# Hybrid encoder layer with routed experts: the gate's weights loaded in the order of their use, and half a gather in other PSUM banks

## The chip, the cores and the metric

The kernel runs on one core of one Trainium2 chip. The metric is the device time of one execution in microseconds; lower is better. The engines are named as in the profile: PE is TensorE (PEld its weight loads), DVE is VectorE, ACT is ScalarE, POOL is GpSimd, SP is SyncE, which computes nothing and here issues the loads.

## The reference, cut to what matters

One layer over 256 tokens of width 2048, all in 32-bit floats. An input projection, attention and a state-space scan, an output projection and a layer norm come first; the change does not touch them. Then:

```
def routed_experts(x, w_router, router_bias, w_gate, w_up, w_down):
    ...                                     # sigmoid router, best group, top 2 of 16 experts per token
    for e in range(N_EXPERTS):
        hid = jax.nn.silu(xt @ w_gate[e]) * (xt @ w_up[e])
        out = out + combine[:, e:e + 1] * (hid @ w_down[e])
...
def per_layer_embedding(x, p_i, w_ple, w_ple_gate):
    gate = jax.nn.sigmoid(jnp.einsum('bsd,de->bse', x, w_ple_gate))
    return gate * jnp.einsum('bsk,kd->bsd', p_i, w_ple)
...
        h = layer_norm(DEEPNORM_ALPHA * h + moe + ple, ln2_g[i], ln2_b[i])
```

There are 16 experts with a hidden width of 1024: w_gate and w_up of an expert are 2048 x 1024 (8 MB each), w_down is 1024 x 2048 (8 MB). w_ple_gate is 2048 x 2048 (16 MB), w_ple is 256 x 2048 (2 MB).

## The kernel before, in words

After the first layer norm the transposed activations lie in `hT`, and the kernel walks through the experts 0 to 15. Each expert has room for 64 of the 256 tokens (`CAP`); tokens beyond that are counted, and an overflow loop behind a branch handles them. Per expert:

- `gate_up(e, xg)` (L724): the gathered tokens against w_gate and w_up, 8 tiles of 2 MB, 16 matmul instructions each;
- `hidden` (L734 to L750): silu and product, transposes; in its gaps stand the two halves of `return_half` of the expert before (L763 matmuls into banks named `bk`, then L768 on VectorE, which adds the weighted rows to `acc`). Its bank tags are mt and pl for the first half, gu and mt for the second;
- in experts 2, 4, 5 and 7 `residual` (L911 transposes into pl banks, L913 on VectorE);
- behind odd experts `gather` (L703): one-hot matmuls pick the tokens of the next two experts, into four PSUM tiles of which each is scaled and copied out by ScalarE or VectorE;
- `down(e, hidT)` (L790): 4 tiles of 2 MB; for the last expert `down_last` (L814) takes the weights in four quarters of 32 small DMAs in all;
- behind experts 3, 6, 9 and 12 `ple_gate(c)` (L832, L842): one of four column chunks of the per-layer gate, with 16 blocks of w_ple_gate in three ring tiles of 4, 8 and 4 blocks, the last with the chunk of w_ple.

In expert 7, between `residual` and `gather`, stands `overflow()`: the branch of L857 on a count that is read from memory. In expert 13 the gain and bias of the last norm are spread over the partitions by small matmuls (`row_bank`, L901).

All weights of the experts and of the gate come through one ring of SBUF buffers of 2 MB each (`class Ring`): eight from expert 1 on, and a ninth at the start. `plan_loads` writes the list of loads in order. `take` hands out a tile and puts its buffer in the list of spare ones, and `fill` issues the next loads of the list into spare buffers; both are called as the tiles are consumed, so the n-th load goes into the buffer of the n-8th tile taken, and SyncE waits with its DMA until TensorE has read that tile. SyncE issues in order. One gate chunk is five DMAs: four of 1 MB (L93) in rows of 2 KB, and one of 512 KB (L96). In the list the three tiles of a chunk stand ahead of the gate and up of the expert behind whose down they are used:

```
        if e in PLE_AT:
            c = PLE_AT.index(e)
            L += [(("pg", c, g), gate_part(g, c)) for g in range(3)]
        for k in range(4):
            L.append((("g", e, k), wide(i["w_gate"][0, e], k, R)))
            L.append((("u", e, k), wide(i["w_up"][0, e], k, R)))
```

The order on TensorE is written out by hand: `phase()` puts each of these parts behind the last TensorE instruction of the part before, except right behind the branch.

Of the kernel before, what the change touches and what calls it, by code (L numbers as in the profile page):

```python
# [7 lines left out]
F32 = mybir.dt.float32  # L8
# [10 lines left out]
NE, FE, CAP = 16, 1024, 64  # L19
# [4 lines left out]
WB = 3  # L24
RING0, RING1, RING2, RING3 = 4, 2, 2, 4
R = 4
PLE_AT = (3, 6, 9, 12)
RES_AT = (2, 4, 5, 7)
LN2_AT = 13
PLE_PARTS = ((0, 4), (4, 12), (12, 16))  # L30
# [43 lines left out]
def plan_loads(nc, ring, i):  # L74

    def rows(src, row0, nrow, col0, ncol):
        return lambda t: nc.sync.dma_start(
            t[:, :nrow // 128 * ncol].rearrange("p (k f) -> p k f", f=ncol),
            src[row0:row0 + nrow, col0:col0 + ncol].rearrange("(k p) f -> p k f", p=128))

    def wide(src, b, r):

        return lambda t: nc.sync.dma_start(t, src[b * 128 * r:(b + 1) * 128 * r, :].rearrange("(p r) f -> p (r f)", r=r))

    def gate_part(g, c):

        cs = slice(c * 512, (c + 1) * 512)
        k0, k1 = PLE_PARTS[g]

        def load(t):  # L90
            v = t.rearrange("p (k f) -> p k f", f=512)
            for k in range(k0, k1, R):
                nc.sync.dma_start(v[:, k - k0:k - k0 + R, :],  # L93
                                  i["w_ple_gate"][0][k * 128:(k + R) * 128, cs].rearrange("(p r) f -> p r f", r=R))
            if k1 == KB:
                nc.sync.dma_start(v[:, k1 - k0:k1 - k0 + 2, :], i["w_ple"][0][:, cs].rearrange("(k p) f -> p k f", p=128))  # L96
        return load

    def quarter(src, q):
        def load(t):  # L100
            v = t.rearrange("p (k d f) -> p k d f", d=2, f=256)
            for b in range(4):
                for dh in range(2):
                    nc.sync.dma_start(
                        v[:, 2 * b:2 * b + 2, dh, :],
                        src[b * 256:(b + 1) * 256, dh * 1024 + q * 256:dh * 1024 + (q + 1) * 256]
                        .rearrange("(p r) f -> p r f", r=2))
        return load

    L = ring.loads  # L110
    L.append(("p", rows(i["p"][0, 0], 0, 256, 0, 256)))
    for e in range(NE):
        if e in PLE_AT:
            c = PLE_AT.index(e)
            L += [(("pg", c, g), gate_part(g, c)) for g in range(3)]
        for k in range(4):
            L.append((("g", e, k), wide(i["w_gate"][0, e], k, R)))
            L.append((("u", e, k), wide(i["w_up"][0, e], k, R)))
        if e < NE - 1:
            L += [(("d", e, k), wide(i["w_down"][0, e], k, 2)) for k in range(4)]  # L120
        else:
            L += [(("d", e, q), quarter(i["w_down"][0, e], q)) for q in range(4)]


def front(ctx, tc, i, dbg=lambda *a: None):
# [6 lines left out]
    fr = Front()  # L132
    fr.const, fr.ring, fr.dram = const, ring, dram
    plan_loads(nc, ring, i)

    es_mix, es_xt, es_tm, es_ps = (ExitStack() for _ in range(4))
# [397 lines left out]
def back(ctx, tc, i, out, fr, dbg=lambda *a: None):  # L534
# [4 lines left out]
    psum = ctx.enter_context(tc.tile_pool(name="psum2", bufs=1, space=PSUM))  # L539
# [12 lines left out]
    def mt_psum(shape):  # L552
        return psum.tile(shape, F32, name="mt", tag="mt", bufs=2)
# [39 lines left out]
    for k2 in range(8):  # L593
        ps = banks[k2].rearrange("p (k t) -> p k t", k=2)
# [17 lines left out]
    for k in range(KB):  # L612
        g = k % 4
# [60 lines left out]
    @contextmanager  # L674
    def phase():

        after = tc.issue_after(place[0]) if place[0] else ExitStack()
        with after:
            yield
        place[0] = [i for i in nc.cur_bb.bb.instructions if i.engine == mybir.EngineType.PE][-1]  # L680
# [13 lines left out]
    def gather(oh):  # L694

        xg = mp.tile([128, KB, 2, CAP], F32, name="xg", tag="xg")
        for k4 in range(4):
            ps = mt_psum([128, 4, 2, CAP])
            ks = range(4 * k4, 4 * k4 + 4)
            for k in ks:  # L700
                cols = slice(k * 128, (k + 1) * 128)
                for t in range(NT):
                    nc.tensor.matmul(ps[:, k % 4], h[:, t, cols], oh[:, t], start=t == 0, stop=t == 1)  # L703
            if k4 % 2:
                for k in ks:
                    nc.scalar.activation(xg[:, k], ps[:, k % 4], AF.Identity, bias=lnT[:, 1, k:k + 1],
                                         scale=lnT[:, 0, k:k + 1])
            else:
                b = [128, 4, 2 * CAP]
                v, p = (a.rearrange("p k e c -> p k (e c)") for a in (xg[:, ks.start:ks.stop], ps))  # L710
                gain, bias = (lnT[:, n, ks.start:ks.stop, None].to_broadcast(b) for n in range(2))
                nc.vector.tensor_tensor(v, p, gain, op=OP.mult)
                nc.vector.tensor_tensor(v, v, bias, op=OP.add)
        return xg
# [110 lines left out]
    def ple_gate(c):  # L825
        cs = slice(c * 512, (c + 1) * 512)
        pg = [pl_psum() for _ in range(NT)]
        for g, (k0, k1) in enumerate(PLE_PARTS):
            w = v2(ring.take(("pg", c, g)), 512)
            for k in range(k0, k1):  # L830
                for t in range(NT):
                    nc.tensor.matmul(pg[t], hT[:, k, t * 128:(t + 1) * 128], w[:, k - k0, :],  # L832
                                     start=k == 0, stop=k == KB - 1)
            if k1 < KB:
                ring.fill()
        w = w[:, k1 - k0:k1 - k0 + 2, :]
        for t in range(NT):
            sg = mp.tile([128, 512], F32, name="sg", tag="w2", bufs=1)
            nc.scalar.activation(sg, pg[t], AF.Sigmoid)
            ps = mt_psum([128, 512])  # L840
            for k in range(2):
                nc.tensor.matmul(ps, pT[:, k, t * 128:(t + 1) * 128], w[:, k, :], start=k == 0, stop=k == 1)  # L842
            nc.vector.tensor_tensor(sg, sg, ps, op=OP.mult)
            nc.gpsimd.tensor_tensor(acc[:, t, cs], acc[:, t, cs], sg, op=OP.add)
        ring.fill()
# [48 lines left out]

    oh = onehot(0)
    xg = gather(oh)

    def row_bank(ps, rows, c):
# [17 lines left out]
    for e in range(NE):  # L916
# [18 lines left out]
        if e + 1 < NE:  # L935
            if e % 2:
                with phase():
                    oh = oh_next
                    xg = gather(oh)
            with phase():  # L940
                last = e, cm, down(e, hidT)
        else:
            with phase():
                down_last(e, hidT, cm)
        if e == 0:
# [16 lines left out]
            nc.gpsimd.dma_start(scro, ovT)  # L962
        if e in PLE_AT:
            with phase():
                ple_gate(PLE_AT.index(e))
        if e == LN2_AT:
# [50 lines left out]
```

## Time and profile before

| | us |
|---|---|
| median of 3 runs | 1493.62 |
| lowest and highest run | 1490.85, 1495.37 |
| the profiled execution | 1492.86 |
| its span, first to last instruction | 1490.7 |
| TensorE busy | 1369.6 |
| VectorE busy | 454.1 |
| ScalarE busy | 296.7 |
| GpSimd busy | 62.1 |

The span is that of one profiled execution; 2.2 us of its time lie outside. Busy times of engines overlap and don't add up to the span. The core read 496.68 MB from HBM, 335 GB/s over the span. Experts run from about 460 us to 1471 us.

### The profile page before, as it was taken

How to read it: one execution, taken by the hardware profiler on the slowest of the kernel's cores; microseconds unless marked ns; L12 is line 12 of the kernel's file. 1: busy time of each engine (PE TensorE's matmuls, PEld its weight loads, DVE VectorE, ACT ScalarE, POOL GpSimd, SP SyncE). 2: the span in 40 equal slices, each digit the busy share in tenths (PEclk: the TensorE clock that was granted, in tenths of full speed). 3: DMA queues.
4: the chain of work that ended last, by engine and by line, in shares of the span. 5: the costliest groups of instructions: out<-in, count | busy, mean ns of one | idle time of the engine just before them, and what ended most of it. 6: DMA issues, size and time to landing. Idle time of an engine off the chain costs nothing. (4 is left out here: it accounts for less than half of the span.)

```text
span 1490.7 us, 15640 instructions
## 1 busy us (share of the span) xinstructions
PE 1369.6 (92%) x6595; PEld 741.5 (50%) x6595; DVE 454.1 (30%) x768; ACT 296.7 (20%) x477; POOL 62.1 (4%) x80
## 2 busy tenths in 40 slices
PE   7999999999979999689998899897899988999994
PEld 5877888787765343144334233432443342335332
DVE  4486774545551022020113010320201111011127
ACT  3475554444330010010001000100100010002001
POOL 3000120200000000000000000000000000000002
PEclk9999999999998999899999999999999999999997
DMA  8655545466847999998899999899979999999994
GB/s 265 198 171 169 173 153 186 165 211 253 308 187 319 427 425 426 415 427 361 365 426 414 427 426 383 345 415 424 413 297 422 426 415 427 425 382 385 416 394 149
DMA packets 89647, 499.92 MB, mean 335 GB/s; under 512 B 9684, under 2 KB 22396, under 8 KB 65252
## 3 DMA queue, kind: packets, MB, share of 16 engines
q1 hardware_dynamic: 88128, 495.41, 82.9%
q0 software_dynamic: 1408, 3.41, 0.8%
q8 instruction: 54, 0.88, 0.2%
q14 instruction: 21, 0.17, 0.0%
q10 hardware_dynamic: 36, 0.05, 0.0%
HBM read 496.68 MB, written 2.16 MB: 335 GB/s over the span
## 5 line engine op out<-in xcount | busy, mean ns | idle before, releaser
L724 PE MATMUL pgu<-ring,xg 128*64 128x512 f32 x2048 | 458.5, 604 | 54.7 <-DMA ring<-in_w_gate 38.9
L724 PEld LDWEIGHTS pgu<-ring,xg 128*64 128x64 f32 x2048 | 148.1, 139 | 361.4 <-issue 315.1
L790 PE MATMUL py<-ring,hidT 128*64 128x512 f32 x960 | 210.2, 594 | 4.5 <-DMA ring<-in_w_down 3.5
L207 DVE TENSOR_TENSOR wl<-ring,wh 128x1024 fp32r<-128x1024 f32 x128 | 156.1, 1223 | 141.3 <-ACT wh L206 136.1
L206 ACT ACTIVATE wh<-ring 128x1024 fp32r<-128x1024 f32 x128 | 135.3, 1059 | 173.4 <-PE pj L213 145.0
L211 PE MATMUL pj<-wh,xh 128*128 128x512 f32 x384 | 153.9, 403 | 0.5 <-ACT xh L188 0.3
L212 PE MATMUL pj<-wl,xh 128*128 128x512 f32 x384 | 153.8, 401 | 0.0
L213 PE MATMUL pj<-wh,xl 128*128 128x512 f32 x384 | 152.9, 399 | 0.0
L734 DVE TENSOR_TENSOR hid<-hid,pgu 128x512 f32<-128x512 f32 x16 | 11.0, 687 | 433.2 <-ACT hid L733 433.2
L790 PEld LDWEIGHTS py<-ring,hidT 128*64 128x64 f32 x960 | 67.2, 137 | 137.4 <-issue 126.1
L832 PE MATMUL pl<-ring,hT 128*128 128x512 f32 x256 | 110.9, 594 | 0.0
L733 ACT ACTIVATE hid<-pgu 128x512 f32<-128x512 f32 x16 | 9.6, 597 | 424.5 <-PE pgu L724 424.5
L779 DVE TENSOR_TENSOR y<-py,y 128x512 fp32r<-128x512 f32 (+1 forms) x34 | 22.4, 660 | 220.0 <-ACT y L778 220.0
L703 PE MATMUL mt<-wr,h 128*128 128x128 f32 x512 | 67.5, 299 | 16.1 <-DVE acc L768 7.1
L768 DVE SCALAR_TENSOR_TENSOR acc<-bk,cw,acc 128x512 f32<-128x512 f32 (+1 forms) x128 | 81.7, 711 | 1.9 <-PE bk L763 1.9
L211 PEld LDWEIGHTS pj<-wh,xh 128*128 128x128 f32 x384 | 72.6, 189 | 17.5 <-ACT xh L188 1.5
L213 PEld LDWEIGHTS pj<-wh,xl 128*128 128x128 f32 x384 | 72.7, 189 | 16.5 <-DVE xl L189 0.2
L212 PEld LDWEIGHTS pj<-wl,xh 128*128 128x128 f32 x384 | 72.7, 189 | 16.1
L832 PEld LDWEIGHTS pl<-ring,hT 128*128 128x128 f32 x256 | 48.3, 190 | 62.6 <-issue 62.6
L703 PEld LDWEIGHTS mt<-wr,h 128*128 128x128 f32 x512 | 66.0, 212 | 18.6 <-DVE acc L768 8.9
L778 ACT ACTIVATE y<-py 128x512 fp32r<-128x512 f32 (+1 forms) x34 | 19.4, 572 | 234.6 <-PE py L790 206.0
L212 PE MATMUL pj<-wl,moh 128*128 128x512 f32 (+1 forms) x160 | 56.5, 353 | 0.5 <-DVE wl L207 0.5
(252 smaller groups left out, 933.9 us busy)
## 6 DMA issues: line engine op xcount, KB each, us to landing
ring<-in_w_gate SPq DMA_DIRECT2D x64, 2048.0 KB, 18.9
ring<-in_w_up SPq DMA_DIRECT2D x64, 2048.0 KB, 18.5
ring<-in_w_down SPq DMA_DIRECT2D x60, 2048.0 KB, 20.4
ring<-in_w_in SPq DMA_DIRECT2D x48, 1024.0 KB, 5.1
ring<-in_w_out SPq DMA_DIRECT2D x16, 1024.0 KB, 6.5
ring<-in_w_ple_gate SPq DMA_DIRECT2D x16, 1024.0 KB, 26.2
ring<-in_w_down SPq DMA_DIRECT2D x32, 256.0 KB, 6.0
xq<-in_x SPq DMA_DIRECT2D x8, 256.0 KB, 10.5
```

What stands on the lines that cost most here:

```text
L206: nc.scalar.activation(h, v, AF.Copy)
L207: nc.vector.tensor_tensor(l, v, h.bitcast(F32), op=OP.subtract)
L211: nc.tensor.matmul(ps, ah, bh, start=first, stop=False)
L212: nc.tensor.matmul(ps, ah, bl, start=False, stop=False)
L213: nc.tensor.matmul(ps, al, bh, start=False, stop=last)
L703: nc.tensor.matmul(ps[:, k % 4], h[:, t, cols], oh[:, t], start=t == 0, stop=t == 1)
L724: nc.tensor.matmul(pgu[j][hs], xg[:, k, e % 2, :], w[:, r, fh * 512:(fh + 1) * 512], start=k == 0, stop=k == KB - 1)
L768: nc.vector.scalar_tensor_tensor(a, ps[dh], cw[:, t, e:e + 1], a, op0=OP.mult, op1=OP.add)
L778: nc.scalar.activation(yh, ps, AF.Copy)
L779: nc.vector.tensor_tensor(yl, ps, yh.bitcast(F32), op=OP.subtract)
L790: nc.tensor.matmul(py[hs, c, :], hidT[:, j, fh * 64:(fh + 1) * 64], w[:, r, dh * 1024 + c * 512:dh * 1024 + (c + 1) * 512], start=fb == 0, ...
L832: nc.tensor.matmul(pg[t], hT[:, k, t * 128:(t + 1) * 128], w[:, k - k0, :], start=k == 0, stop=k == KB - 1)
```

## The change

The three tiles of a gate chunk are put in the list of loads behind the down tiles of the expert they follow, so that the list has the order of use. The chunks are behind experts 3, 7, 10 and 12 in place of 3, 6, 9 and 12 (counted from 0). Of gather's four PSUM tiles the first two take the banks with the tag pl, and the last two keep mt.

```
-PLE_AT = (3, 6, 9, 12)
+PLE_AT = (3, 7, 10, 12)
...
     for e in range(NE):
-        if e in PLE_AT:
-            c = PLE_AT.index(e)
-            L += [(("pg", c, g), gate_part(g, c)) for g in range(3)]
         for k in range(4):
             L.append((("g", e, k), wide(i["w_gate"][0, e], k, R)))
             L.append((("u", e, k), wide(i["w_up"][0, e], k, R)))
...
             L += [(("d", e, q), quarter(i["w_down"][0, e], q)) for q in range(4)]
+        if e in PLE_AT:
+            c = PLE_AT.index(e)
+            L += [(("pg", c, g), gate_part(g, c)) for g in range(3)]
...
         for k4 in range(4):
-            ps = mt_psum([128, 4, 2, CAP])
+            ps = psum.tile([128, 4, 2, CAP], F32, name="mt", tag=("pl", "mt")[k4 // 2], bufs=2)
```

## Rows read from the trace of the kernel before

**Rows 1.** The first part of the page: each engine's busy time, share of the span and instructions.

```profile
PE 1369.6 (92%) x6595; PEld 741.5 (50%) x6595; DVE 454.1 (30%) x768; ACT 296.7 (20%) x477; POOL 62.1 (4%) x80
```

**Rows 2.** TensorE's waits between 460 and 1466 us: what waited, for what, the total in us, how many times, the longest.

```profile
PE pgu L724 <- DMA ring<-in_w_gate: 38.9, 14, 13.2
PE pgu L724 <- DMA ring<-in_w_up: 15.8, 13, 1.3
PE mt L703 <- DVE acc L768: 7.1, 5, 1.9
PE mt L703 <- PEq L857: 6.1, 1, 6.1
PE py L790 <- DMA ring<-in_w_down: 3.5, 4, 1.3
```

**Rows 3.** Stretches of the span: from:to, length, then busy us and instructions of PE, PEld, DVE, ACT and POOL, and last the granted TensorE clock, the DMA engines' busy share and the GB/s they moved.

```profile
471.00:575.00 104.00, 101.10 (x522) 40.19 (x520) 14.72 (x26) 8.34 (x18) 0.62 (x1) 1.00 1.01 426
536.90:544.40 7.50, 7.48 (x66) 7.36 (x68) 3.72 (x7) 1.50 (x4) 0.00 (x0) 1.00 1.00 426
575.00:655.00 80.00, 60.13 (x280) 20.36 (x275) 11.10 (x17) 3.26 (x6) 0.00 (x0) 0.91 1.01 421
600.30:612.30 12.00, 3.87 (x20) 1.11 (x16) 1.38 (x2) 1.19 (x2) 0.00 (x0) 0.83 1.06 401
697.00:718.00 21.00, 21.00 (x62) 8.56 (x62) 1.38 (x2) 1.19 (x2) 2.52 (x2) 1.00 0.55 201
900.00:910.00 10.00, 10.00 (x34) 3.85 (x34) 1.38 (x2) 1.19 (x2) 2.54 (x2) 1.00 0.70 264
952.00:962.00 10.00, 10.00 (x58) 4.96 (x59) 1.38 (x2) 1.97 (x6) 0.00 (x0) 1.00 0.37 125
1062.20:1071.40 9.20, 9.13 (x66) 9.01 (x68) 3.77 (x8) 1.50 (x4) 0.00 (x0) 0.81 1.00 424
1090.00:1120.00 30.00, 30.00 (x80) 12.75 (x80) 1.37 (x2) 1.19 (x2) 2.53 (x2) 1.00 0.66 258
1300.00:1314.00 14.00, 14.00 (x45) 5.57 (x45) 1.38 (x2) 1.19 (x2) 3.50 (x4) 1.00 0.77 304
1374.00:1382.00 8.00, 8.00 (x36) 2.42 (x34) 0.00 (x0) 0.00 (x0) 0.00 (x0) 0.86 0.54 186
```

**Rows 4.** TensorE in order of time, experts 2 to 4 and the start of 10 and 11: start, length, line, operation and shapes, in brackets the idle time before and what ended it.

```profile
558.12 27.64 PE L724 MATMUL pgu<-ring,xg 128*64 128x512 f32 x128
590.22 13.95 PE L790 MATMUL py<-ring,hidT 128*64 128x512 f32 x64
...
651.64 3.65 PE L724 MATMUL pgu<-ring,xg 128*64 128x512 f32 x16 [1.25 <-DMA ring<-in_w_up]
...
682.04 27.73 PE L832 MATMUL pl<-ring,hT 128*128 128x512 f32 x64
713.14 27.69 PE L724 MATMUL pgu<-ring,xg 128*64 128x512 f32 x128
...
1116.29 27.69 PE L724 MATMUL pgu<-ring,xg 128*64 128x512 f32 x128
...
1161.20 27.64 PE L724 MATMUL pgu<-ring,xg 128*64 128x512 f32 x128
```

**Rows 5.** SyncE's issues in order of time, around the first chunk: start, the time that the issuing took, line and DMA.

```profile
575.50 24.01 SPq L93 DMA_DIRECT2D ring<-in_w_ple_gate  x4
...
602.16 1.18 SPq L83 DMA_DIRECT2D ring<-in_w_gate  x1
...
689.21 0.33 SPq L83 DMA_DIRECT2D ring<-in_w_up  x1
702.94 0.33 SPq L83 DMA_DIRECT2D ring<-in_w_gate  x1
713.24 0.33 SPq L83 DMA_DIRECT2D ring<-in_w_up  x1
```

**Rows 6.** The loads that L83 issues between 700 and 715 us, from issue to landing.

```profile
DMA to landing us min/median/max: 7.9/7.9/7.9
```

**Rows 7.** The branch's line on SyncE and on TensorE's sequencer: how many, the shortest, median and longest in ns, first and last start in us.

```profile
L857 SPq EVENT_SEMAPHORE  x8: 17/17/17, 945.1 to 955.1; - x8
L857 PEldq COMPARE_BRANCH  x1: 6172/6172/6172, 938.1 to 938.1; - x1
```

**Rows 8.** TensorE in order of time: the first instruction behind gate and up of expert 7, and the first of expert 8.

```profile
933.99 1.19 PE L763 MATMUL bk<-y,cm 64*128 64x512 f32 x8
...
968.28 27.64 PE L724 MATMUL pgu<-ring,xg 128*64 128x512 f32 x128
```

**Rows 9.** TensorE before and at the gather of expert 9, VectorE's accumulations at the same time, and VectorE's residual of expert 5, in order of time.

```profile
1059.13 1.19 PE L763 MATMUL bk<-y,cm 64*128 64x512 f32 x8
1062.27 9.11 PE L703 MATMUL mt<-wr,h 128*128 128x128 f32 x64 [1.95 <-DVE acc L768]
...
1057.52 5.36 DVE L768 SCALAR_TENSOR_TENSOR acc<-bk,cw,acc 128x512 f32<-128x512 f32 x8
...
792.69 2.08 DVE L913 SCALAR_TENSOR_TENSOR acc<-pl,acc 128x512 f32<-128x512 f32 x2
```

**Rows 10.** TensorE in order of time: the start of the last chunk's matmuls as far as the asked stretch goes, and the last quarter of the last down.

```profile
1278.47 21.73 PE L832 MATMUL pl<-ring,hT 128*128 128x512 f32 x50
...
1465.70 3.67 PE L814 MATMUL py<-ring,hidT 128*64 128x256 f32 x32
```

## The prediction

> **What bounds the kernel now.** I read the page first. TensorE is busy for 92% of the span [rows 1], which looks like the bound, but pipelined matmuls make that share hard to read. So I went to TensorE's waits in the expert stretch, 460 to 1466 us [rows 2]. It waited 38.9 + 15.8 + 3.5 = 58.2 us for weights that were still being loaded, 7.1 us for VectorE's accumulations, and 6.1 us once at the branch of the overflow code. So weights are what it lacks. The third view asks whether the DMA engines were full all that time [rows 3]. In long stretches they move 421 to 426 GB/s at a share of 1.0, the most that any row of the page shows. But in six short stretches they don't. Against 425 GB/s the lost DMA time is length x (1 - rate/425): 697 to 718 loses 11.1 us, 900 to 910 3.8, 952 to 962 7.1, 1090 to 1120 11.8, 1300 to 1314 4.0, 1374 to 1382 4.5; together 42.2 us. Four of the six lie at the four chunks of the per-layer gate (at 682 to 713 for the first, [rows 4]), one at the overflow branch, one near the end.
>
> So the expert stretch is bound by DMA, and its engines stop now and then because no buffer is free. While the first chunk runs, SyncE issues a load only as the chunk's parts are consumed: 689.2, 702.9, 713.2 us [rows 5]. That is the wait to read the change by.
>
> **A rule for the loss, checked on the old order.** The ring has eight 2 MB buffers; a load goes out when the tile eight takes earlier has been read. A tile is 2.10 MB / 426 GB/s = 4.92 us. A load into an idle queue lands after 7.9 us [rows 6], so a restart costs 7.9 - 4.9 = 3.0 us. A chunk holds TensorE for 713.14 - 682.04 = 31.1 us, and hands back its three buffers 6.9, 20.7 and 31.1 us after its start [rows 4, 5]. Let L be the lead: how long before a chunk starts the last down tile ahead of it has landed. In the old order the chunk's three tiles were loaded a whole expert earlier and sit in three buffers, so behind that down tile the queue has five buffers and the first two that the chunk frees: 7 x 4.92 = 34.4 us. The third can restart it at L + 31.1 + 0.1 + 3.0 = L + 34.2. Loss = L - 0.2.
>
> Where the gate and up before was starved, the last up tile is picked up as it lands. For expert 3 that is 651.6; the chunk starts 30.4 us later, the four down tiles take 19.7, so L = 10.7 and the loss 10.5 (measured 11.1). Behind expert 9 the same, with a gather 1.6 us slower: 12.1 (measured 11.8). Behind 6 and 12 even the down tiles were awaited, L = 3.5, loss 3.3 (measured 3.8 and 4.0). Four chunks, 29.2 by the rule and 30.7 by the trace.
>
> **The change, part by part.**
>
> *Loads behind the down.* No transfer is added or removed. The 20 DMAs of the four chunks (16 gate, 4 projection) move on SyncE's queue past the twelve loads of their expert; POOL's queue is untouched. Loads now stand in the order of use, so the chunk itself is still on its way when the last down tile has landed: 4.72 MB at 401 GB/s is 11.8 us [rows 3]. Loss = L - 12.0, or nothing below that.
>
> *Chunk behind expert 3 (index as in the code).* Its gate and up are starved (expert 2 ends at 604, and 39.4 us of tiles face 27.6 us of matmuls), so L is 10.7 again, or 8.8 with the gather's wait gone. Loss 0, with 1.3 to 3 us to spare. The 13.2 us wait before expert 3 [rows 2], when TensorE sat behind the chunk's transfer, shrinks as well.
>
> *From there to the second chunk.* After a chunk the lead is L + 31.1 - 11.8, some 28 to 30. An expert's twelve tiles need 59 us. TensorE needs 44.9 for an even expert (1116.29 to 1161.20), 46.0 with a residual (558.12 to 604.17), 54.4 for an odd one [rows 4]. The lead goes to about 16, 11 and then under zero: expert 6 is starved, and so is the gate and up of 7.
>
> *Chunk behind expert 7, past the overflow branch.* From the end of gate and up to the end of the down is 968.28 - 933.99 = 34.3 us there [rows 8], the 6.2 us branch included [rows 7]; with the last up tile's own 3.6 us, less 19.7, L = 18.2. And SyncE drains: after the branch it passes eight waits between 945.1 and 955.1 us, the last as the last load lands [rows 7], and issues nothing before. In the new order the last load ahead of the branch is the first gate tile of expert 8, which lands 11.8 + 4.9 us after the down tiles, 1.5 us before the chunk starts. Restart: 0.4 + 3.0 = 3.4 us lost. Then four down buffers and two parts of the chunk, 6 x 4.92 = 29.5 us, last to 31.4 us into the chunk, and the third part restarts at 34.2: 2.8 lost. Together 6.2 us, in place of 7.1 for the branch alone now.
>
> *Chunks behind 10 and 12.* By the same ledger the lead is 17 after expert 8, 11 after 9, and 10 is starved: L = 3.5, loss 0. Then 23, 16 after 11, about 2 after 12: starved again, loss 0. The 4.5 us at 1374 go too: a full ring stood still there while TensorE was at LN2's row banks; by the ledger the lead behind expert 13 is about 27 us, of the 39 that eight buffers can hold.
>
> *Half of the gather in other banks.* Gather's first bank now waits for the seventh of eight VectorE accumulations: matmuls end at 1060.3, it starts at 1062.27, 1.9 us [rows 9]; and two of those gathers then ran 1.6 us longer: a granted clock of 0.81 in the one at 1062, in part the level of 1.2 GHz, after that pause, against 1.00 (2.4 GHz) in the one at 537 [rows 3]. The pl banks are free after the fourth accumulation, about 1060.2. Gain 1.9 us at experts 1, 3, 9 and 11, and up to 3.3 of clock: at most 11 us of TensorE time. At expert 5 the residual's two VectorE operations (792.69 to 794.8) hold pl instead: about 1.7 us worse, where the first operation ends at 793.8. All of it lies behind DMA, so it counts nothing in the sum; without that cover it would be -9 us. Bounds: -9 and +2.
>
> **Sum.** 42.2 - 6.2 = 36.0 us. The rule came out 1.5 us low over four chunks, so I take 35. Does TensorE become the bound at the end? Its work from the last chunk on runs without a wait for weights today, from 1278.47 [rows 10]. That chunk would start 11.8 (its own transfer no longer stands ahead) + 33.8 (the first four losses) - 6.2 = 39.4 us earlier, so TensorE alone would end at 1490.7 - 39.4 = 1451.3, and DMA, at 1490.7 - 35 = 1455.7, ends last. The tail behind the last quarter of the down, 1490.7 - 1465.7 = 25.0 us, stays. The profiled execution has 2.2 us outside its span and lies 0.8 us under the median of the runs, so 1455.7 + 2.2 + 0.8 = 1458.7 us.
>
> **A rate from the Trainium skill.** Two stretches of 80 and 104 us ran at 421 and 426 GB/s [rows 3]. The Trainium skill's page "HBM Reference", section "Specifications (TRN2)", gives a core a share of about 358 GB/s when both cores of a pair stream, and says that one alone measures about 425. By the share, the 401 MB behind 471 us would take some 1120 us where 994 are used now, an estimate from that page; the trace agrees with the figure for a core alone.
>
> **Rivals.**
> *Slower: issuing the chunk starves the queue.* SyncE spent 24.0 us on four gate DMAs, against 0.3 for a weight tile [rows 5], and can issue nothing else meanwhile. If the queue ran dry behind each, every chunk could cost up to 24 us, 4 x 24 - 35 = 61 slower (1555); it decides from 35/4 = 8.8 us a chunk on, and at 11 a chunk the time is 1503. For it: the chunk now comes when the queue is short. Against it: in 575 to 655, with that issue inside, the DMA share is 1.01 [rows 3], and the same four down tiles stand ahead of it. 5 in 100.
> The Trainium skill's page "Perfetto Trace Analysis", section 'What "DMA-bound" means', names this case: an issuing engine solid with DMA slices is the bound. Here the slices are solid, but the engines behind them are full, so the trace does not bear it out.
> *The branch costs more.* If the drain kept SyncE from issuing until the second chunk has freed its last buffer, the queue would stand 34 us in place of 6: 1487. If TensorE had to wait out SyncE's drain too, some 22 us: 1481. Today TensorE left the branch at 944.4 while SyncE drained to 955.1 [rows 7], which speaks against it. 9 in 100.
> *No change.* TensorE, not DMA, would have to set the time. 58 us of its waits are for DMA, so it can't hold over the whole stretch; 3 in 100, at 1493.6.
> *More than forecast.* The join costs nothing and TensorE's end decides: 1451 to 1454. 8 in 100.
>
> **How the numbers follow.** The forecast has 75 in 100, by itself 1454 to 1466 (a few microseconds of idle where 1.3 us of slack runs out, and 4 us of TensorE surprise hidden). The range 1451 to 1471 takes in the better case and small excess at the branch. A change of 0.3%, 4.5 us, is about what a measurement of this kernel can tell from none. Faster: 75 + 8 + 9 = 92; same 3; slower 5.
>
> **What would show it.** Right: the DMA rate stays at 420 or more through the chunks behind 3, 10 and 12; one gap of 3 to 4 us after the branch and one of about 3 at the end of the chunk behind 7; TensorE's waits for the ring fall from 58 to 30 to 45 us and lie in experts 3, 6, 7, 10 and 15; gathers start without the 1.9 us wait, except behind the residual of 5. Wrong: a DMA gap behind the gate issues, TensorE waiting at the branch until SyncE has drained, or no ring wait left at the end.

## The result and the profile after

| | before | after |
|---|---|---|
| median of the runs, us | 1494.21 (4 runs) | 1453.22 (4 runs) |
| lowest and highest run, us | 1490.85, 1495.37 | 1453.09, 1454.92 |
| the profiled execution, us | 1492.86 | 1453.28 |
| its span, us | 1490.7 | 1451.2 |

The ratio is 0.9732, with a 95% interval of 0.9714 to 0.975: faster by 2.7%. The forecast was 1458.7 us with a range of 1451 to 1471; the time came out 5.5 us below the forecast, inside the range. A second set of runs of the same kernel gave 1453.0 us and 0.9731 [0.9717, 0.9744].

The first part of the page after, beside [rows 1]: each engine runs as many instructions as before, and TensorE's share rose although its busy time fell by 11.2 us, because the span shrank by 39.5.

```profile
PE 1358.4 (94%) x6595; PEld 735.2 (51%) x6595; DVE 453.5 (31%) x768; ACT 296.9 (20%) x477; POOL 62.1 (4%) x80
```

TensorE's waits from 460 to 1430 us, beside [rows 2] (what waited, for what, total us, times, longest):

```profile
PE pgu L724 <- DMA ring<-in_w_up: 18.2, 16, 1.3
PE pgu L724 <- DMA ring<-in_w_gate: 14.9, 13, 1.3
PE py L790 <- DMA ring<-in_w_down: 6.4, 7, 1.3
PE mt L703 <- PEq L857: 6.1, 1, 6.1
...
PE mt L703 <- DVE acc L768: 0.9, 1, 0.9
```

The waits for weights fell from 58.2 to 18.2 + 14.9 + 6.4 = 39.5 us. The 13.2 us wait is gone: the longest left for weights is 1.3. Of the gathers' waits for VectorE, 7.1 us, one of 0.9 is left. TensorE still lacks weights, but each time only by the little that a full queue brings them late.

Whether the queue is full is to be seen in stretches of the span, beside [rows 3] (from:to, length, busy us and instructions of PE, PEld, DVE, ACT and POOL, granted clock, DMA share, GB/s):

```profile
471.00:575.00 104.00, 103.04 (x530) 40.78 (x528) 14.54 (x26) 8.35 (x18) 0.62 (x1) 1.00 1.01 427
655.00:700.00 45.00, 45.00 (x140) 18.12 (x138) 2.76 (x4) 2.40 (x4) 2.01 (x2) 1.00 1.02 417
700.00:900.00 200.00, 177.25 (x894) 67.76 (x890) 40.95 (x64) 12.48 (x26) 0.52 (x1) 1.00 1.01 427
920.00:932.00 12.00, 12.00 (x42) 4.63 (x39) 1.38 (x2) 1.20 (x2) 0.00 (x0) 1.00 0.66 251
952.00:962.00 10.00, 10.00 (x39) 3.62 (x39) 1.38 (x2) 1.20 (x2) 2.53 (x2) 1.00 0.86 336
1100.00:1140.00 40.00, 38.70 (x108) 15.86 (x106) 2.76 (x4) 2.39 (x4) 1.89 (x2) 1.00 1.02 415
1230.00:1270.00 40.00, 38.65 (x108) 15.86 (x106) 2.07 (x3) 2.35 (x4) 2.25 (x3) 1.00 1.02 416
1320.00:1345.00 25.00, 25.00 (x132) 13.90 (x130) 1.39 (x2) 5.76 (x10) 0.00 (x0) 0.86 1.01 427
1345.00:1399.00 54.00, 53.26 (x262) 18.56 (x260) 8.08 (x12) 2.67 (x5) 0.00 (x0) 1.00 1.01 427
```

Through the chunks behind experts 3, 10 and 12 (655 to 700, 1100 to 1140, 1230 to 1270) the engines are full; the 415 to 417 GB/s at a share of 1.02 are the chunk's own slower rows of 2 KB, which moved at 401 in [rows 3]. The stretch behind LN2's row banks, which lost 4.5 us from 1374 to 1382 before, now lies some 40 us earlier and is full too (1320 to 1345), like the one behind it. Two gaps are left, where the forecast put them: 920 to 932, behind the overflow branch, and 952 to 962, at the end of the chunk behind expert 7.

### The profile page after: what moved, and what is told of

Read it like the earlier page. It is cut to its first block, busy times and chain, and to the rows that moved or that the text cites. A ratio compares the mean times of both kernels' runs of the same rounds, so it can differ in the third digit from the quotient of the medians.

```text
span 1451.2 us, 15673 instructions
## 1 busy us (share of the span) xinstructions
PE 1358.4 (94%) x6595; PEld 735.2 (51%) x6595; DVE 453.5 (31%) x768; ACT 296.9 (20%) x477; POOL 62.1 (4%) x80
## 5 line engine op out<-in xcount | busy, mean ns | idle before, releaser
L724 PE MATMUL pgu<-ring,xg 128*64 128x512 f32 x2048 | 450.2, 595 | 33.1 <-DMA ring<-in_w_up 18.2
L779 DVE TENSOR_TENSOR y<-py,y 128x512 fp32r<-128x512 f32 (+1 forms) x34 | 22.5, 660 | 223.8 <-ACT y L778 223.8
L703 PE MATMUL mt<-wr,h 128*128 128x128 f32 x512 | 64.0, 289 | 7.9 <-PEq L857 6.1
L703 PEld LDWEIGHTS mt<-wr,h 128*128 128x128 f32 x512 | 62.5, 204 | 10.3 <-PEq L857 6.3
## 6 DMA issues: line engine op xcount, KB each, us to landing
ring<-in_w_down SPq DMA_DIRECT2D x60, 2048.0 KB, 25.8
```

The source lines that it names most:

```text
L724: nc.tensor.matmul(pgu[j][hs], xg[:, k, e % 2, :], w[:, r, fh * 512:(fh + 1) * 512], start=k == 0, stop=k == KB - 1)
L779: nc.vector.tensor_tensor(yl, ps, yh.bitcast(F32), op=OP.subtract)
```

## The experiments

**The parts alone.** Four kernels divide the change: the new order of the loads alone, the new places alone, the new banks alone, and the whole change without the banks.

The order alone, as an edit of the kernel after:

```
-PLE_AT = (3, 7, 10, 12)
+PLE_AT = (3, 6, 9, 12)
...
-            ps = psum.tile([128, 4, 2, CAP], F32, name="mt", tag=("pl", "mt")[k4 // 2], bufs=2)
+            ps = mt_psum([128, 4, 2, CAP])
```

> The loads in the order of use alone: chunks behind 3, 6, 9 and 12 as before, gather in its old banks. Theory (order): the old order lost 30.7 us at the chunks because three buffers held a chunk for a whole expert; with the order alone the loss at the chunks is L - 12.0, L about 10.7 behind 3, 12.3 behind 9, 3.5 behind 6 and 12, so almost nothing, and the branch costs one restart of 3 us with no chunk right behind it. 1449 to 1455 us. Rival (TensorE): the pauses before the gathers and the slower clock set a good part of the time; without the new banks it is 9 to 11 us above the changed kernel, 1462 to 1464. Rival (places): the chunk must stand behind 7 and 10; at 1465 or above if that is worth a third of the gain.

Measured: 1452.34 us, ratio 0.9735 [0.9719, 0.9752], the same as the whole change. Stretches of its span, columns as above; the overflow branch is in the second, and the third is the end of the chunk behind expert 3, where the first gap of [rows 3] stood:

```profile
900.00:930.00 30.00, 24.01 (x148) 15.16 (x145) 11.53 (x18) 2.98 (x7) 0.00 (x0) 0.89 1.01 423
930.00:950.00 20.00, 20.00 (x98) 7.03 (x98) 1.56 (x3) 2.70 (x6) 0.00 (x0) 1.00 0.80 322
690.00:712.00 22.00, 22.00 (x76) 8.44 (x76) 1.38 (x2) 1.19 (x2) 2.53 (x2) 1.00 1.00 416
```

One gap is left, behind the branch: 20 x (1 - 322/425) = 4.8 us. The order alone carries a gain as large as the whole. The rivals by which TensorE or the places would have held part of it fall.

The places alone, as an edit of the kernel before:

```
-PLE_AT = (3, 6, 9, 12)
+PLE_AT = (3, 7, 10, 12)
```

> Only the chunks' places are new (behind 3, 7, 10 and 12); loads in the old order, gather in its old banks. Theory (order): nothing gained, since a chunk still holds three buffers for an expert; the chunk behind 7 now stands right after the branch's drain, so its loss is not smaller: 1492 to 1498 us. Rival (places): below 1485.

Measured: 1492.49 us, ratio 1.0002 [0.999, 1.0013]. The places do nothing in the old order.

The banks alone, as an edit of the kernel before:

```
-            ps = mt_psum([128, 4, 2, CAP])
+            ps = psum.tile([128, 4, 2, CAP], F32, name="mt", tag=("pl", "mt")[k4 // 2], bufs=2)
```

> Only the gather's banks are new, loads and places as before. Theory (order): in the old order the loss at a chunk is L - 0.2, and L falls by the 1.9 us wait (and 1.6 of clock) behind the odd experts 3 and 9, so this edit, which should be nearly worthless in the new order, gains some 5 to 9 us in the old: 1485 to 1489 us, with a smaller DMA gap at the chunks behind 3 and 9 and unchanged ones behind 6 and 12. Rival (TensorE): every pause counts, 9 to 11 us: 1483 to 1485, DMA gaps smaller everywhere. If it is hidden here too: 1492 to 1496.

Measured: 1486.01 us, ratio 0.9952 [0.9935, 0.997]. Its stretches at the chunks behind experts 3, 6 and 9, beside [rows 3]:

```profile
695.00:716.00 21.00, 21.00 (x64) 8.53 (x64) 1.38 (x2) 1.19 (x2) 2.52 (x2) 1.00 0.64 239
898.00:908.00 10.00, 10.00 (x35) 3.72 (x35) 1.38 (x2) 1.20 (x2) 2.54 (x2) 1.00 0.69 259
...
1086.00:1116.00 30.00, 30.00 (x83) 12.58 (x83) 1.38 (x2) 1.19 (x2) 2.54 (x2) 1.00 0.72 284
```

In the old order a faster gather did count, and the rule for the loss says where: a gather stands between the last up tile's pick-up and the chunk only behind odd experts, and only there does a faster gather shorten the lead L. Behind 3 the loss is 21 x (1 - 239/425) = 9.2 us in place of 11.1, behind 9 it is 30 x (1 - 284/425) = 10.0 in place of 11.8; behind 6, with no gather ahead of the chunk, it is 3.9, as before (3.8). That is the size of the rule behind 3 (1.9 us) and half of it behind 9, where it has 3.5. These two account for 3.7 us. The span of the profiled execution fell by 5.0, of which 1.2 is an earlier start of the first expert (458.69 us in place of 459.86). The runs fell by more, 6 to 7 us (1486.01 against a median of 1492.18 in the same set, and by the ratio); what lies beyond the 5.0 no profile here shows.

The whole change without the banks, as an edit of the kernel after:

```
-            ps = psum.tile([128, 4, 2, CAP], F32, name="mt", tag=("pl", "mt")[k4 // 2], bufs=2)
+            ps = mt_psum([128, 4, 2, CAP])
```

> The changed kernel with the gather back in its old banks. Theory (order): hidden behind DMA, 0 to 2 us above the changed kernel's 1453.2: 1453 to 1455. Rival (TensorE): 9 to 11 above, 1462 to 1464.

Measured: 1455.29 us, ratio 0.9753 [0.9737, 0.977], just over the expected stretch; the interval overlaps that of the kernel after. Its profiled span is 1451.9. Its waits from 460 to 1430 us:

```profile
PE pgu L724 <- DMA ring<-in_w_up: 11.9, 10, 1.3
PE pgu L724 <- DMA ring<-in_w_gate: 10.3, 9, 1.3
PE mt L703 <- DVE acc L768: 7.1, 5, 1.9
PE mt L703 <- PEq L857: 5.8, 1, 5.8
PE py L790 <- DMA ring<-in_w_down: 3.6, 4, 1.3
PE mt L703 <- DVE acc L770: 1.9, 1, 1.9
```

TensorE waits 25.8 us for weights in place of 39.5, 13.7 less, and the span is 0.7 us longer: it spends about as much more on its own, 8.1 us in the gathers' waits for VectorE (7.1 + 1.9 in place of 0.9) and 5.8 in slower gathers (L703 is busy for 69.8 us in place of 64.0). That is the cover of which the prediction spoke, seen from the other side: once the DMA engines are full, what TensorE saves it waits out again. The banks are worth 6 to 7 us where gaps stand behind a lead, and some 2 us (1455.29 against 1453.22), not told from nothing by the intervals, where none does.

**The places in the new order.** An edit of the kernel after:

```
-PLE_AT = (3, 7, 10, 12)
+PLE_AT = (3, 6, 9, 12)
```

> The changed kernel (order of use, new banks) with the chunks back behind 3, 6, 9 and 12. Theory (order): the chunk behind 7 costs about 2 us of DMA at its end, since the ring had only just restarted after the branch; without it there the branch costs its restart of 3 us alone. 1449.5 to 1453.5 us, 0 to 3 under the changed kernel's 1453.2. Rival (places): 1457 or above.

Measured: 1453.68 us, ratio 0.9742 [0.9721, 0.9764], just over the expected stretch and not to be told from the kernel after. The places are neutral here too.

**The branch.** The overflow loop is left out of both kernels:

```
-OV_AT = 7
+OV_AT = 99
```

> The changed kernel without the overflow branch (the loop for tokens beyond an expert's capacity is left out). Theory: the branch costs DMA 3 us of restart and 2 us at the end of the chunk behind it, and TensorE 6.1 us that lie behind DMA; 1447 to 1450 us, both DMA gaps gone. Rival: the branch costs only TensorE's 6.1 us, or nothing: 1453.

Measured from the kernel after: 1448.19 us, ratio 0.97 [0.9676, 0.9723], 5.0 us less than after. Stretches of its span:

```profile
905.00:935.00 30.00, 30.00 (x101) 11.80 (x98) 1.38 (x2) 1.35 (x3) 0.00 (x0) 1.00 1.03 414
935.00:965.00 30.00, 30.00 (x110) 11.33 (x110) 1.38 (x2) 1.20 (x2) 2.54 (x2) 1.00 1.00 421
```

> The kernel before without the overflow branch (the same loop left out). Theory: its 7 us of DMA gap at 952 to 962 goes, the four gaps at the chunks and the one at 1374 stay: 1484 to 1487 us. Rival (only TensorE's 6.1 us count and these are hidden): 1491 or above.

Measured from the kernel before: 1486.95 us, ratio 0.9959 [0.9948, 0.9969]. Stretches of its span, around expert 7 and at the chunk behind expert 3:

```profile
940.00:960.00 20.00, 19.57 (x122) 11.46 (x124) 5.95 (x10) 3.01 (x8) 0.00 (x0) 1.00 1.00 421
698.00:719.00 21.00, 21.00 (x62) 8.56 (x62) 1.38 (x2) 1.19 (x2) 2.52 (x2) 1.00 0.57 205
```

Without the branch both gaps of the kernel after close, the one at the end of the chunk behind 7 too, which the prediction had put down to the branch and the drain. In the old order the gap of the branch closes and that of the chunk stays: 21 x (1 - 205/425) = 10.9 us. The two causes are separate, and the change took away one and left most of the other. The edit also takes away TensorE's 6.1 us at the branch, so the time by itself doesn't say which of the two counted. That it was the DMA is read from the closed gaps and from TensorE's waits for weights, which rose from 39.5 to 41.2 us without the branch.

**The rule of the lead, one buffer less.** If the losses are a matter of buffers, a ring of seven in place of eight takes 4.92 us from each lead that the ring can cover:

```
-RING0, RING1, RING2, RING3 = 4, 2, 2, 4
+RING0, RING1, RING2, RING3 = 4, 2, 2, 3
```

> The changed kernel with seven ring buffers in place of eight. Theory (buffers): one tile less ahead, so the first restart at 456 us comes 5 us sooner in the queue and is lost, the chunk behind 3 has no slack left (L - 7 in place of L - 12: about 1.5 us lost), the one behind 7 loses about 5 us more, those behind 10 and 12 nothing: 10 to 13 us over the changed kernel, 1463 to 1466. Rival (the lead does not matter once loads stand in order of use): within 5 us of the start's loss, under 1459.

Measured: 1467.0 us, ratio 0.9827 [0.9804, 0.985], 13.8 us more than after and 1 us over the expected stretch. The start of the experts in the kernel after, and then that start, the end of the chunk behind expert 3 and that of the chunk behind expert 7 with seven buffers:

```profile
450.00:470.00 20.00, 20.00 (x118) 12.17 (x118) 3.01 (x6) 3.02 (x8) 0.00 (x0) 0.93 0.58 229
```

```profile
450.00:470.00 20.00, 20.00 (x114) 12.85 (x116) 3.82 (x12) 3.01 (x8) 0.00 (x0) 0.89 0.32 117
700.00:712.00 12.00, 12.00 (x50) 4.21 (x50) 1.38 (x2) 0.60 (x1) 2.53 (x2) 1.00 0.93 369
950.00:970.00 20.00, 20.00 (x65) 7.77 (x65) 1.38 (x2) 1.19 (x2) 2.53 (x2) 1.00 0.76 295
```

At the start the loss grows by 20 x (229 - 117)/425 = 5.3 us, about the time of the missing buffer's 2 MB. Behind expert 3, where the forecast had 1.3 to 3 us to spare with eight, 12 x (1 - 369/425) = 1.6 us appear. At the end of the chunk behind 7 it is 20 x (1 - 295/425) = 6.1 us, where the kernel after lost 10 x (1 - 336/425) = 2.1. Together 10.9 of the 13.8. Another 20 x (1 - 358/425) = 3.2 us are lost from 1340 to 1360, behind LN2's row banks, where the expectation had nothing.

> The kernel before with seven ring buffers in place of eight. Theory (buffers): the rule with one buffer less is L + 4.7 lost at each chunk in place of L - 0.2, up to the 17 us or so that the chunk's own parts allow, one tile less ahead at the start (5 us), and the same again where the row banks stop the ring: 17 to 25 us over the kernel before, 1510 to 1518, against the 14 us that the same edit cost in the order of use. Rival (the buffers that a chunk holds for an expert are not what costs): about 14 us here too, 1505 to 1508.

Measured on the kernel before with the same edit: 1515.45 us, ratio 1.0145 [1.0126, 1.0163], 22.3 us more than before in the same set (1493.15). Stretches at the first chunk and ahead of it:

```profile
700.00:726.00 26.00, 26.00 (x75) 10.62 (x75) 1.38 (x2) 1.20 (x2) 2.52 (x2) 1.00 0.60 228
670.00:690.00 20.00, 20.00 (x111) 10.02 (x110) 2.13 (x4) 3.61 (x9) 0.00 (x0) 0.99 0.77 311
```

At the chunk behind 3 alone the loss is now 26 x (1 - 228/425) = 12.1 us, and ahead of it stands a gap of 20 x (1 - 311/425) = 5.4 that eight buffers didn't have: the tiles loaded early take up three buffers of seven. The rule has 4.9 us more at each chunk. Counted in the same way over wider stretches, so that the gaps ahead are in them, the loss grew by 6.3, 4.4, 5.1 and 5.0 us at the chunks behind 3, 6, 9 and 12 (670 to 730, 900 to 920, 1080 to 1140 and 1310 to 1340 with seven buffers; 670 to 730, 900 to 910, 1070 to 1130 and 1300 to 1320 with eight). So the old order is the more sensitive to the ring's size, as the rule has it.

**The kernel after once more**, without an edit, beside the one with seven buffers in the old order:

> The changed kernel once more, beside the kernel before, for the size of what differs between runs of one kernel: 1452 to 1456 us; the start of the first expert, which the change doesn't touch, anywhere between 457.5 and 461.5 us.

Measured: 1453.0 us; its first expert starts at 458.39 us, where the first profile of the same kernel has 458.25. No kernel tried that computes everything is faster than the change by more than the runs can tell.

## Why the prediction was right, and where 5.5 us were

*DMA bound, with gaps where no buffer is free.* Right. The order of the loads alone gives the whole 2.7%, and taking a buffer away brings gaps back in both orders.

*Loss = L - 12.0 in the new order, nothing at the chunks behind 3, 10 and 12.* Right in all three, and the margin behind 3 was as small as forecast: with seven buffers 1.6 us are lost there.

*6.2 us at expert 7.* Right in place and nearly in size. By the rate the gaps lose 12 x (1 - 251/425) = 4.9 and 2.1 us, together 7.0; by the DMA share (12 x 0.34 + 10 x 0.14) it is 5.5. The landings tell it more closely, a 2 MB tile being 4.90 us behind the one before it while the queue is full: from 924.75 two tiles took until 937.61, 3.1 us more than 9.8, and from 957.21 one took until 964.07, 2.0 more, together 5.0 where the forecast had 3.4 + 2.8. Without the branch 5.0 us go. SyncE's drain is seen in the line of the branch after, beside [rows 7], and in SyncE's issues, beside [rows 5]:

```profile
L857 SPq EVENT_SEMAPHORE  x8: 17/17/17, 916.6 to 924.8; - x8
...
L857 PEldq COMPARE_BRANCH  x1: 6172/6172/6172, 894.7 to 894.7; - x1
```

```profile
875.92 30.88 SPq L93 DMA_DIRECT2D ring<-in_w_ple_gate  x4
906.86 2.49 SPq L96 DMA_DIRECT2D ring<-in_w_ple  x1
909.45 1.18 SPq L83 DMA_DIRECT2D ring<-in_w_gate  x1
924.90 0.34 SPq L83 DMA_DIRECT2D ring<-in_w_up  x1
```

The last load ahead of the branch is the first gate tile of expert 8, as the prediction had it, and the next goes out at 924.90, 0.1 us behind the eighth wait, long before the chunk's last buffer is free (956.35, by the issue that waits for it). TensorE left the branch at 894.7 + 6.2 = 900.9, 24 us before SyncE: it did not wait for the drain. So both forms of the rival, 1487 and 1481 us, fell. The Trainium skill's page "Runtime: NRT & Kernel Launch", section "Instruction fetch mechanics", says that a taken branch to a page that isn't prefetched makes the sequencer fetch it and stall. That would fit the 6.17 us, which are the same in both kernels, but no run here tells this from another cause.

*Issuing the chunk starves the queue.* Refuted in the rows above: the stretch of four gate DMAs on SyncE is 30.88 us, longer than the 24.01 in [rows 5], and the DMA share of 700 to 900 is 1.01. Some of either stretch is a wait for a buffer: the four DMAs by themselves are 26.4 us, one of them 17.84, in place of 21.1. That a full queue is what holds SyncE there fits the share, but no run tests it. The Trainium skill's page "Perfetto Trace Analysis", section 'What "DMA-bound" means', counts an issuing engine that is solid with DMA slices as a bound; here, as in the forecast, the trace does not bear that out.

*Banks hidden.* Right for the change: some 2 us, by the kernel without them. The bounds of -9 and +2 held for the banks alone too (-6 to -7). The time of TensorE that is covered was put at 11 us at most, by the old order: in the new one, without the banks, it is some 14, since there four gathers run slowly, at 9.0 to 9.1 us, and not two. One detail was wrong: the gather of expert 5 was to start 1.7 us later behind the residual's VectorE operations, and it waited 0.92 us, about as long as before (0.89).

```profile
778.37 7.53 PE L703 MATMUL mt<-wr,h 128*128 128x128 f32 x64 [0.92 <-DVE acc L768]
```

The other gathers have no wait for VectorE. Why the residual did not hold this one was not followed up; at a full queue it costs nothing either way.

*Waits for the ring of 30 to 45 us.* 39.5, in experts 3, 6, 7, 10 and 15 as forecast, and also at the ends of 2 and 5 and in 12.

*The sum.* The profiled span fell by 39.5 us where 35 were forecast. The term of the DMA is right: the last weights land at 1428.73 in place of 1464.96, 36.2 us earlier, of which 1.6 is the start of the first expert (458.25 in place of 459.86); 34.6 are left. That start lies ahead of all that the change touches and varied from 457.7 to 461.2 us over the profiles of this study, so I put these 1.6 us down to chance; it isn't shown, since the only two profiles of one kernel lie 0.1 us apart.

The term that was mis-sized is the tail. "The tail behind the last quarter of the down, 25.0, stays" put the DMA's gain on the end of TensorE, as if the last quarter's matmuls could not start before the weights were there. From the last landing to the end of the span it was 1490.7 - 1464.96 = 25.7 us before and is 1451.2 - 1428.73 = 22.5 after: 3.3 us. The chain that ended last shows how, in pieces from the wait for the last up tile to the last quarter (start us, us, what):

```profile
1377.20 26.21 DMA ring<-in_w_up
1403.42 0.04 issue
1403.46 3.65 PE pgu L724 x16
...
1420.73 3.63 PE py L814 x32
...
1425.78 4.08 PE py L814 x32
```

The last weights come with the DMAs of L104, first the three issued from 1419.8 to 1421.3 us, then the last one of the kernel before, with the time from issue to landing:

```profile
L104 SPq DMA_DIRECT2D ring<-in_w_down x3: 540/540/540, 1419.8 to 1421.3; - x3
...
DMA to landing us min/median/max: 7.4/7.5/7.5
```

```profile
L104 SPq DMA_DIRECT2D ring<-in_w_down x1: 540/540/540, 1459.1 to 1459.1; - x1
...
DMA to landing us min/median/max: 5.9/5.9/5.9
```

The last lands at 1421.28 + 7.45 = 1428.73, 3.0 us after the quarter's matmuls have begun (1425.71 in the order of time). A quarter is eight DMAs, and TensorE takes them as they come: its matmuls took 4.14 us in place of 3.67 [rows 10]. In the kernel before, TensorE was the later by 0.74 us (1465.70 [rows 10] against 1459.11 + 5.85 = 1464.96), so the weights could come 0.74 + 3.02 us later against the matmuls at a price of 0.47; that is the 3.3. With -0.4 at the DMA, +1.6 at the start and +3.3 at the tail the 4.5 us between 35 and 39.5 are told. Most of the last 1 us up to 5.5 is between runs: the prediction added 0.8 for the median over the profiled execution, and after the median lies 0.06 below it.

So the rival "more than forecast", TensorE's end decides, came true at the end of the kernel, by another way than it named. By the prediction's own stretches the 1453.2 us are that rival's (1451 to 1454, 8 in 100) and lie just under those of the forecast (1454 to 1466); the range held because it took the rival in. That the rival's number was met is in part luck: the join at expert 7, which it put at nothing, did cost its 5 us, but behind the last chunk, which started 40.6 us earlier (1237.83 in place of 1278.47), TensorE waited for weights only 2.0 of its 39.5 us. The two ends, which the prediction put 4.4 us apart, lie within these few.

Two readings in the prediction were off without moving its sum. The page before has slices of 427 GB/s, so 426 is not the most that it shows. And the 54.4 us of an odd expert stand in no row that it names; the trace has 558.12 - 503.83 = 54.3 for expert 1.

## What to carry to other kernels

In a ring of buffers, put the loads in the order of their use: a tile that is loaded early takes a buffer away from the queue for all the time between, and what it costs can be read beforehand as length x (1 - rate/full rate) of the stretches where the engines stop. A saving on an engine behind a full queue (here 13.7 us of TensorE for some 2 us of time, not told from nothing) is worth little there, though the same edit was worth 6 to 7 us while the queue had gaps, so gains of parts don't add up. Where two ends are within a few microseconds, look at the grain in which the last consumer takes its data before you add a fixed tail to the later one.

## What the runs showed of the hardware

- SyncE's issuing of a DMA in rows of 2 KB can take long without any loss: 26.4 us for four of 1 MB, in a stretch of 30.88, at a DMA share of 1.01.
- At the branch's join SyncE lets all loads in flight land before it issues again: 8.2 us from the first to the eighth wait (916.6 to 924.8). The last load in flight, the gate tile, lands at 909.45 + 15.30 = 924.75, just ahead of the eighth. TensorE left after 6.17 us on its own.
- The last down's small DMAs moved 333 to 352 GB/s at a share of 1.05 to 1.09, against 427 for the 2 MB tiles. From 1410 to 1425 us, columns as in the stretches above:

```profile
1410.00:1415.00 5.00, 4.52 (x42) 2.69 (x38) 3.48 (x6) 0.85 (x3) 0.00 (x0) 1.00 1.09 352
1415.00:1420.00 5.00, 4.52 (x44) 2.76 (x42) 3.35 (x10) 0.39 (x1) 0.00 (x0) 1.00 1.06 340
1420.00:1425.00 5.00, 4.52 (x42) 2.75 (x42) 3.35 (x10) 0.38 (x1) 0.00 (x0) 1.00 1.05 333
```
